# A step of two elements in the stationary operand of an up projection's matmuls

## The chip, the cores and the metric

The kernel runs on one core of a Trainium2 chip. The metric is the device time of one execution in microseconds (us). TensorE (PE) does the matmuls and, as instructions of their own, the loads of the stationary operand (PEld in the profile); VectorE is DVE, ScalarE is ACT, GpSimd is POOL, SyncE is SP.

## The reference

The program is two layers of an encoder on 256 tokens of width 2048. Each layer is an input projection, two kinds of attention, an output projection, and then the part that this case is about, a gated feed-forward block of width 5632:

```python
D_MODEL = 2048; SEQ = 256; DEPTH = 2; D_FF = 5632
def depthwise_conv(u, w, bias):
    up = jnp.pad(u, ((0, 0), (1, 1), (0, 0)))
    return up[:, :-2] * w[0] + up[:, 1:-1] * w[1] + up[:, 2:] * w[2] + bias
...
for l in range(DEPTH):
    h = rms_norm(x, ln1_g[l])
    proj = h @ w_in[l]
    ...                                  # two groups of attention heads
    x = x + o @ w_out[l]
    h2 = rms_norm(x, ln2_g[l])
    u = depthwise_conv(h2 @ w_up[l], conv_w[l], conv_b[l])
    gate, up = u[..., :D_FF], u[..., D_FF:]
    x = x + (jax.nn.silu(gate) * up) @ w_down[l]
```

All arrays are float32. `w_up` is 2048 x 11264: its first 5632 columns give the gate, the others the value that is gated.

## The kernel before, in words

**Numbers in two parts.** TensorE reads float32 operands in a type called float32r here. To keep the precision, every operand is split into a high part (the value written as float32r, by ACT) and a low part (the rest, by DVE). A product is then taken as high x high + low x high + high x low.

**Quanta and steps.** The weights come from DRAM in quanta of 128 partitions x 2048 float32. A quantum is worked on in steps, of which each takes a half of 1024 elements a partition: SP issues a DMA into a tile `raw`, ACT writes the high part `whi` from it (line 1002), DVE the low part `wlo` (line 1011); for some halves a DMA that adds, issued by POOL, makes the low part in the tiles `v_a` and `v_b` instead (line 988). Some high parts lie in a tile named `kT`. All of these copies go over the 1024 elements in a row, whatever they mean. Splits run four steps ahead of the matmuls.

**The up projection.** For each of 44 blocks f of 128 columns (of the gate and of the value) there are two quanta u, so four steps; in two layers 2 x 44 x 4 = 352 steps. One step holds, for four blocks kk of 128 input rows, the 128 columns of the gate (j = 0) and the 128 columns of the value (j = 1). `q_up` gives TensorE 8 pairs of matmuls in a step, one pair for each j and kk. In a pair the weights are the stationary operand and the tile `xs` is the moving one; `xs` holds the high part of 128 input rows x 256 tokens and behind it the low part. The function `two` makes the pair: high weights with all 512 columns of `xs` (128 x 512), then low weights with the 256 columns of its high part (128 x 256). So a step is 16 matmuls, each with a load of its own, and the widths 512 and 256 alternate. The stationary operand is 128 partitions x 128 float32, before the change in a row (512 bytes of a partition).

**Other matmuls.** The input, output and down projections have activations as stationary and weights as moving operand, 512 columns wide throughout (`three`, `q_seven`, `q_plain`, `q_down`).

**What sets the order.** In the feed-forward part the class `Plan` puts the operations of ACT, DVE, POOL and PE in order from costs and due times that stand in the code; outside it a scheduler does. Both go by sizes and not by where a matmul reads its operands. After the up matmuls of a block, `glu` on ACT and DVE reads the sums from PSUM and does the convolution, the gate and the splits.

**Where the weights lie.** `place` puts the split weights of an up step 56 elements into their tile (`UP_AT`). `_layout` arranges the weights on the host, ahead of the run.

Of the kernel before, what the change touches and what calls it, by code (L numbers as in the profile page):

```python
# [18 lines left out]
P = 128  # L19
L = 2  # L20
# [11 lines left out]
NF = FF // P  # L32
# [94 lines left out]
def encoder_kernel(  # L127
# [370 lines left out]
    def two(ps, w_h, w_l, mv, first, last):  # L498

        mm(ps, w_h, mv, first, False)  # L500
        mm(ps[:, 1], w_l, mv[:, 0], False, last)
# [121 lines left out]
    def q_up(l, f, u):  # L623
        def body(q, half, hi, lo):
            if u == 0 and half == 0:
                cur["up"] = psum.tile([P, 2, 2, T], F32, name="mm", bufs=2)
            ps = cur["up"]
            hv, lv = (w.rearrange("p (k j n) -> p k j n", k=4, j=2) for w in (hi, lo))
            for j in range(2):
                for kk in range(4):  # L630
                    k = 8 * u + 4 * half + kk
                    two(ps[:, j], hv[:, kk, j], lv[:, kk, j], xs[k], k == 0, k == KD - 1)
            if u == 1 and half == 1:
                glu(l, f, q, ps)
        return body
# [247 lines left out]
    for l in range(L):  # L883
# [7 lines left out]
        f = 0  # L891
# [363 lines left out]
def _layout(inputs):  # L1255
    f = {k: np.asarray(v) for k, v in inputs.items()}
    c = np.ascontiguousarray
    o = {}
    rows = T // GRID_W

    down = np.arange(T).reshape(rows, GRID_W).T.reshape(-1)
    o["x"] = c(f["x"][0][down].reshape(TT, P, D).transpose(1, 0, 2))
    o["xT"] = c(f["x"][0][down].T.reshape(KD, P, T).transpose(1, 0, 2))
    o["pos"] = c(f["positions"][down].reshape(TT, P).T)
    d = HD
    inv = np.float32(10000.0) ** (-np.arange(0, d, 2, dtype=np.float32) / np.float32(d))
    o["inv"] = inv.astype(np.float32)
    ln_g = np.stack([f["ln1_g"], f["ln2_g"]]).reshape(2, L, KD, P).transpose(3, 0, 1, 2)
    o["head"] = c(np.concatenate([ln_g.reshape(P, -1), o["xT"][:, :2].reshape(P, -1)], 1))
    o["qk_g"] = c(np.stack([f["qn_a"], f["kn_a"], f["qn_b"], f["kn_b"]], 1))  # L1270
    o["sink"] = c(f["sink"].reshape(-1))
    o["on_g"] = c(np.stack([f["on_a"], f["on_b"]], 1).reshape(L, 2, NH, P).transpose(3, 0, 1, 2))
    conv = np.concatenate([f["conv_w"], f["conv_b"][:, None]], 1)
    o["conv"] = c(conv.reshape(L, 4, 2 * NF, P).transpose(3, 0, 1, 2))
    w = f["w_in"]
    qa, ka, va, qb = (w[:, :, i * 1024:(i + 1) * 1024] for i in range(4))
    kvb = w[:, :, 4096:]
    h = slice(0, 512), slice(512, 1024)
    js = {"kvb": kvb, "qb0": qb[..., h[0]], "qb1": qb[..., h[1]], "va0": va[..., h[0]], "va1": va[..., h[1]],
          "ka0": ka[..., h[0]], "ka1": ka[..., h[1]], "qa0": qa[..., h[0]], "qa1": qa[..., h[1]]}  # L1280
    wi = np.stack([js[j] for j in JOBS], 1)
    o["w_in"] = c(wi.reshape(L, NJ, 4, 4, P, 512).transpose(0, 1, 2, 4, 3, 5)).reshape(L, NJ, 4, P, 2048)
    o["w_out"] = c(f["w_out"].reshape(L, 2, 2, 4, P, NB, 512).transpose(0, 1, 5, 2, 4, 3, 6)).reshape(
        L, 2, NB, 2, P, 2048)
    o["w_up"] = c(f["w_up"].reshape(L, 2, 8, P, 2, NF, P).transpose(0, 5, 1, 3, 2, 4, 6)).reshape(
        L, NF, 2, P, 2048)
    wd = f["w_down"]
    n = NF // PART

    four = wd[:, :n * PART * P].reshape(L, n, PART // 2, 2, P, 2, 2, 512).transpose(0, 1, 5, 2, 3, 4, 6, 7)  # L1290
    o["w_seven"] = c(np.stack([four[:, :, :, :, k, :, m] for k, m in ((1, 1), (0, 0), (0, 1), (1, 0))], 5)).reshape(
        L, n, 2, PART // 2, P, 2048)
    o["w_plain"] = c(four[:, :, :, :, 1, :, 0].transpose(0, 1, 2, 4, 3, 5)).reshape(L, n, 2, P, 2048)
    o["w_down"] = c(f["w_down"].reshape(L, NF // FG, FG, P, NB, 512).transpose(0, 1, 4, 3, 2, 5)).reshape(
        L, NF // FG, NB, P, 2048)

    r, cc = np.arange(T) // GRID_W, np.arange(T) % GRID_W
    wr = min(WIN_R, rows)
    r0 = np.clip(r - wr // 2, 0, rows - wr)
    c0 = np.clip(cc - WIN_C // 2, 0, GRID_W - WIN_C)  # L1300
    inside = ((cc[None] >= c0[:, None]) & (cc[None] < c0[:, None] + WIN_C)
              & (r[None] >= r0[:, None]) & (r[None] < r0[:, None] + wr))
    dr = np.clip(r[None] - r[:, None], -(WIN_R - 1), WIN_R - 1) + WIN_R - 1
    dc = np.clip(cc[None] - cc[:, None], -(WIN_C - 1), WIN_C - 1) + WIN_C - 1
    bias = np.full((L, NH, T, T), NEG, np.float32)
    bias[:, :, inside] = f["rpb"][:, :, dr[inside], dc[inside]]

    bias = bias[:, :, down][:, :, :, down]
    bias = np.stack([bias[:, :, tt * P:(tt + 1) * P, tt * (T - KW):tt * (T - KW) + KW] for tt in range(TT)], 2)
    o["bias"] = c(bias.transpose(0, 1, 3, 2, 4))  # L1310
    i = np.arange(T)
    mb = np.where(np.abs(i[:, None] - i[None]) <= WINDOW, np.float32(0), np.float32(NEG))
    mb = mb[down][:, down]
    o["mask_b"] = c(mb.reshape(TT, P, T).transpose(1, 0, 2).astype(np.float32))
    return o
# [19 lines left out]
```

## Time and profile before

| | |
|---|---|
| median of 3 runs (lowest to highest) | 2070.07 us (2069.88 to 2070.23) |
| the profiled execution | 2070.64 us, its span 2068.9 us |
| PE, busy share of the span | 100% |
| PEld, DVE, ACT, POOL | 86%, 82%, 75%, 8% |
| granted TensorE clock | 1.000 |

Matmuls are pipelined, and the profile models their ends, so that PE's share says only that it never stands long without work. The distance from one matmul's start to the next one's tells what one costs. Loads (PEld) overlap the matmuls; a load's recorded duration holds its latency too, so that two loads can overlap each other in the record.

### The profile page before, as it was taken

What the parts mean: (1) busy time and instruction counts of PE and PEld (TensorE: products, weight loads), DVE (VectorE), ACT (ScalarE), POOL (GpSimd) and SP (SyncE); (2) the same over time, 40 slices, a digit from 0 to 9 for tenths busy, and PEclk for the clock granted to TensorE, in tenths of its full rate; (3) what the DMA queues carried; (4) which work ended last, traced back from release to release, by engine and by line L of the source; (5) the groups of instructions that cost most, each with busy time, mean ns of one, the idle gap of its engine ahead of it and who ended that gap; (6) DMA issues with size and microseconds to landing.
All of it is one profiled execution on the core that took longest, in us unless ns stands there. A gap on an engine that the chain in (4) does not pass through costs nothing.

```text
span 2068.9 us, 30510 instructions
## 1 busy us (share of the span) xinstructions
PE 2062.4 (100%) x10720; PEld 1769.9 (86%) x10720; DVE 1706.1 (82%) x2576; ACT 1549.3 (75%) x2595; POOL 157.6 (8%) x170
## 2 busy tenths in 40 slices
PE   9999999999999999999999999999999999999999
PEld 8888888888888888888888888888888888888887
DVE  7786655889999999999757866558899999999995
ACT  7566646988888888888555665479888888888883
POOL 0011000000000000000000111000000000000000
PEclk9999999999999999999999999999999999999999
DMA  9655557888888888898655555678788888888883
GB/s 350 204 163 163 171 180 200 256 233 249 256 265 251 257 251 259 250 263 255 219 181 177 173 166 164 191 211 242 239 251 258 254 256 264 256 252 259 253 261 131
DMA packets 134009, 472.48 MB, mean 228 GB/s; under 512 B 15328, under 2 KB 17888, under 8 KB 133856
## 3 DMA queue, kind: packets, MB, share of 16 engines
q1 hardware_dynamic: 117872, 413.87, 61.2%
q0 software_dynamic: 15264, 55.58, 15.0%
q8 instruction: 84, 1.38, 0.3%
q10 hardware_dynamic: 720, 1.08, 0.2%
q14 instruction: 69, 0.57, 0.1%
HBM read 412.80 MB, written 2.10 MB: 201 GB/s over the span
## 4 chain that ended last, share of the span: by engine, by line
PE 99%; DMA 0%; ACT 0%; ACTq 0%; DVE 0%; issue 0%
PE mm L165 85%; PE S L165 6%; PE pv L165 4%; PE tr L165 3%; PE tr L460 1%; PE tr L381 1%; PE S L220 1%; DMA mid<-in_xT 0%; ACT v_a L335 0%; ACT whi L1002 0%; ACT mid L182 0%; ACT xs L182 0%; DVE x L872 0%; ACTq L1105 0%; ACTq L1098 0%
## 5 line engine op out<-in xcount | busy, mean ns | idle before, releaser
L165 PE MATMUL mm<-xs,whi 128*128 128x512 f32 x2320 | 810.0, 390 | 0.0
L1011 DVE TENSOR_TENSOR wlo<-raw,whi 128x1024 fp32r<-128x1024 f32 x503 | 613.0, 1220 | 185.0 <-ACT whi L1002 162.4
L1002 ACT ACTIVATE whi<-raw 128x1024 fp32r<-128x1024 f32 x569 | 596.2, 1055 | 222.2 <-PE mm L165 182.8
L165 PE MATMUL mm<-xs,wlo 128*128 128x256 f32 x2112 | 596.2, 282 | 0.0
L165 PEld LDWEIGHTS mm<-xs,whi 128*128 128x128 f32 x2320 | 435.3, 188 | 92.1 <-ACT prob L651 0.6
L165 PEld LDWEIGHTS mm<-xs,wlo 128*128 128x128 f32 x2112 | 399.0, 189 | 3.7
L165 PE MATMUL mm<-whi,xs 128*128 128x512 f32 x1152 | 294.8, 393 | 0.8 <-ACT whi L179 0.7
L165 PE MATMUL mm<-whi,mid 128*128 128x512 f32 x928 | 255.2, 393 | 0.4 <-ACT v_a L335 0.4
L165 PEld LDWEIGHTS mm<-whi,xs 128*128 128x128 f32 x1152 | 212.7, 188 | 43.5 <-ACT whi L179 1.3
L165 PEld LDWEIGHTS mm<-whi,mid 128*128 128x128 f32 x928 | 169.9, 188 | 34.3 <-ACT v_a L335 0.9
L165 PE MATMUL mm<-xs,kT 128*128 128x512 f32 x496 | 174.6, 390 | 0.0
L165 PE MATMUL mm<-wlo,xs 128*128 128x512 f32 x576 | 158.7, 392 | 0.0
L667 ACT ACTIVATE pT<-halo,conv 128x256 f32<-128x256 f32 x352 | 157.8, 498 | 0.0
L165 PE MATMUL mm<-wlo,mid 128*128 128x512 f32 x486 | 152.7, 393 | 0.0
L651 ACT ACTIVATE prob<-mm 128x512 f32<-128x512 f32 x176 | 103.6, 591 | 50.2 <-PE mm L165 49.8
L692 DVE TENSOR_TENSOR pT<-pT 128x512 f32<-128x512 f32 x176 | 120.8, 686 | 10.7 <-ACT pT L665 4.3
L165 PEld LDWEIGHTS mm<-wlo,xs 128*128 128x128 f32 x576 | 107.1, 188 | 21.5
L165 PEld LDWEIGHTS mm<-xs,kT 128*128 128x128 f32 x496 | 93.1, 188 | 19.5
L165 PEld LDWEIGHTS mm<-wlo,mid 128*128 128x128 f32 x486 | 90.9, 188 | 19.1
L665 ACT ACTIVATE pT<-halo,conv 128x256 f32<-128x256 f32 x176 | 103.7, 590 | 0.0
L165 PE MATMUL mm<-xs,v_a 128*128 128x256 f32 x352 | 99.3, 282 | 0.0
L165 PE MATMUL mm<-xs,v_b 128*128 128x256 f32 x352 | 99.3, 282 | 0.0
(251 smaller groups left out, 3043.1 us busy)
## 6 DMA issues: line engine op xcount, KB each, us to landing
raw<-in_w_up SPq DMA_DIRECT2D x262, 512.0 KB, 5.6
raw<-in_w_in SPq DMA_DIRECT2D x142, 512.0 KB, 4.4
raw<-in_w_seven SPq DMA_DIRECT2D x110, 512.0 KB, 5.9
raw<-in_w_out SPq DMA_DIRECT2D x64, 512.0 KB, 3.8
tabs<-in_w_up SPq DMA_DIRECT2D x48, 512.0 KB, 5.7
aux<-in_w_up SPq DMA_DIRECT2D x42, 512.0 KB, 5.5
v_a<-raw POOLq DMA_DIRECT2D x39, 512.0 KB, 6.5
v_b<-raw POOLq DMA_DIRECT2D x39, 512.0 KB, 6.5
```

Of the source, the lines that this page charges most:

```text
L165: nc.tensor.matmul(ps, lhsT, rhs, start=start, stop=stop, skip_group_check=True)
L220: nc.tensor.transpose(ps[:, j, tt * P:(tt + 1) * P], x[:, tt, (k + j) * P:(k + j + 1) * P], ident)
L381: nc.tensor.transpose(ps[:, j, tt * P:(tt + 1) * P], qn[tt][:, p + j, :], ident)
L460: nc.tensor.transpose(ps[:, kt, tt * P:(tt + 1) * P], p[:, tt, kt * P:(kt + 1) * P], ident)
L651: nc.scalar.activation(own[part], ps[:, :, part], AF.Copy)
L665: nc.scalar.activation(own["y"][:, j], src, AF.Identity, scale=taps[j][i], bias=taps[j][3])
L667: nc.scalar.activation(own[name][:, j], src, AF.Copy, scale=taps[j][i])
L692: lambda n=n: nc.vector.tensor_add(own["y"], own["y"], own[n]),
L1002: highs[s] = nc.scalar.activation(his[s], source(s), AF.Copy)
L1011: nc.vector.tensor_sub(los[s], source(s), his[s].bitcast(F32))
```

## The change

In the host's layout, the 256 elements that hold one block kk in a half were 128 columns of the gate and behind them 128 of the value. Now they are gate, value, gate, value, in turns. `q_up` reads its operands accordingly: the stationary operand of j starts at element j of the 256 and goes on in steps of two elements (8 bytes), over 1024 bytes of a partition in place of 512.

```diff
@@ q_up
             ps = cur["up"]
-            hv, lv = (w.rearrange("p (k j n) -> p k j n", k=4, j=2) for w in (hi, lo))
+            hv, lv = (w.rearrange("p (k n j) -> p k j n", k=4, j=2) for w in (hi, lo))
             for j in range(2):
                 for kk in range(4):
                     k = 8 * u + 4 * half + kk
                     two(ps[:, j], hv[:, kk, j], lv[:, kk, j], xs[k], k == 0, k == KD - 1)
@@ _layout
-    o["w_up"] = c(f["w_up"].reshape(L, 2, 8, P, 2, NF, P).transpose(0, 5, 1, 3, 2, 4, 6)).reshape(
+    o["w_up"] = c(f["w_up"].reshape(L, 2, 8, P, 2, NF, P).transpose(0, 5, 1, 3, 2, 6, 4)).reshape(
         L, NF, 2, P, 2048)
```

The built program has the same instructions in the same order on every engine, PE, DVE, ACT, POOL and SP. The products, and the order in which they are added up, are the same. What differs is the step of the stationary operand in the up projection's matmuls and the order of the numbers in `in_w_up`.

## The prediction

> **What bounds the kernel.** I read the page first: the shares of the engines, the granted clock by slices, and the shares of the chain that ended last.
>
> ```profile
> span 2068.9 us, 30510 instructions
> ...
> PE 2062.4 (100%) x10720; PEld 1769.9 (86%) x10720; DVE 1706.1 (82%) x2576; ACT 1549.3 (75%) x2595; POOL 157.6 (8%) x170
> ...
> PEclk9999999999999999999999999999999999999999
> ...
> PE 99%; DMA 0%; ACT 0%; ACTq 0%; DVE 0%; issue 0%
> ```
>
> PE carries 99% of the chain, at the full clock in every slice: what a matmul costs decides, and nothing else does while DVE (82%) and ACT (75%) keep up. Loads are as many as matmuls, 10720.
>
> Next, how many of them the change touches. The groups by line and shape of PEld show the up projection's loads as those with `xs` beside a tile that holds weights; `kT`, `v_a` and `v_b` hold such weights too in these stages.
>
> ```profile
> L165 PEld LDWEIGHTS mm<-xs,whi 128*128 128x128 f32 x2320 | 435.3, 188 | 92.1 <-ACT prob L651 0.6
> L165 PEld LDWEIGHTS mm<-xs,wlo 128*128 128x128 f32 x2112 | 399.0, 189 | 3.7
> ...
> L165 PEld LDWEIGHTS mm<-xs,kT 128*128 128x128 f32 x496 | 93.1, 188 | 19.5
> ...
> L165 PEld LDWEIGHTS mm<-xs,v_a 128*128 128x128 f32 x352 | 66.5, 189 | 0.0
> L165 PEld LDWEIGHTS mm<-xs,v_b 128*128 128x128 f32 x352 | 66.5, 189 | 0.0
> ```
>
> High weights: 2320 + 496 = 2816. Low weights: 2112 + 352 + 352 = 2816. That is 352 steps x 8 pairs, by the code too; 5632 loads in all. A recorded 188 ns with its latency doesn't say what a load holds up, so I looked at starts in the timeline, here one pair of an up step:
>
> ```profile
> 340.06 0.39 PE L165 MATMUL mm<-xs,whi 128*128 128x512 f32 x1
> 340.06 0.19 PEld L165 LDWEIGHTS mm<-xs,wlo 128*128 128x128 f32 x1
> 340.29 0.28 PE L165 MATMUL mm<-xs,wlo 128*128 128x256 f32 x1
> 340.29 0.19 PEld L165 LDWEIGHTS mm<-xs,whi 128*128 128x128 f32 x1
> 340.41 0.39 PE L165 MATMUL mm<-xs,whi 128*128 128x512 f32 x1
> ```
>
> The load of the low weights starts together with the 512-wide matmul and has 0.23 us until its own matmul starts; the load of the high weights starts with the 256-wide matmul and has only 0.12 us. So a high load has the thin cover.
>
> Exact distances come from long pieces of the chain, in which PE went from matmul to matmul without a wait (start, length, what):
>
> ```profile
> 10.30 65.60 PE mm L165 x288
> ...
> 75.90 0.44 PE tr L381 x4
> ...
> 338.70 81.25 PE mm L165 x468
> ```
>
> The first is the input projection, 512 columns wide throughout: 65.60 / 288 = 227.8 ns a matmul. The last is the up projection: 468 matmuls are 234 pairs, 81.25 / 234 = 347.2 ns a pair. So a 256-wide matmul takes 347.2 - 227.8 = 119.4 ns.
>
> **The change part by part.** It removes and adds no instruction and moves none: the order on all five engines is the same. DMAs bring the same bytes in the same pieces. The two copies that split the weights go over 1024 elements in a row, as before:
>
> ```profile
> L1011 DVE TENSOR_TENSOR wlo<-raw,whi 128x1024 fp32r<-128x1024 f32 x503 | 613.0, 1220 | 185.0 <-ACT whi L1002 162.4
> L1002 ACT ACTIVATE whi<-raw 128x1024 fp32r<-128x1024 f32 x569 | 596.2, 1055 | 222.2 <-PE mm L165 182.8
> ```
>
> Their 1220 and 1055 ns stay, so those terms are zero. If PE gets slower they only wait longer for free tiles (182.8 us of ACT's idle time there is already a wait for PE); if it gets faster, ACT's 75% and DVE's 82% leave room for some per cent. The whole question is what the 5632 loads cost when they go over 1024 bytes of a partition in steps of 8.
>
> *Term 1, the load beside its cover.* How long does a load occupy its path? The nearest row is where matmuls one column wide follow each other, so that only the loads are left:
>
> ```profile
> 248.45 0.55 PEld L165 LDWEIGHTS pv<-ones,acc_b 128*128 128x128 f32 x4
> ...
> 248.91 0.30 PEld L165 LDWEIGHTS S<-kT,qT 128*128 128x128 f32 x2
> ```
>
> Four loads in 248.91 - 248.45 = 0.46 us, 115 ns each. (These are plain f32 loads; the float32r ones have the same 188 ns in the record, and I take 115 for them too.) Beside 119.4 ns that leaves 4 ns. Lower end: the load takes one element in each of its cycles whether they touch or not, and nothing changes, 0. Upper end: it takes twice as long, 230 ns, and sticks out by 230 - 119.4 = 111 ns under each of 2816 256-wide matmuls, 311 us, and by 2 ns under the 512-wide ones, 6 us: +317 us. Between them I go by pace: the moving operand of a 512-wide matmul is 2048 bytes of a partition in 227.8 ns, 9.0 bytes a ns, so that TensorE does read at this pace; 1024 bytes in 115 ns are 8.9. The strided load asks for no more than the moving operand gets. I take 0 for this term.
>
> *Term 2, what a load takes from the matmul it lies under.* Is the matmul beside a load slower? From 512 to 256 columns the distance falls by 227.8 - 119.4 = 108.4 ns, 0.423 ns a column; 512 columns are then 216.8 ns, and 11.0 ns of each matmul do not depend on its width. A second stretch, of neighbouring down and up matmuls, gives the same by other rows:
>
> ```profile
> 412.86 0.39 PE L165 MATMUL mm<-xs,whi 128*128 128x512 f32 x1
> ...
> 418.41 0.39 PE L165 MATMUL mm<-xs,whi 128*128 128x512 f32 x1
> ...
> 419.79 0.62 PE L165 MATMUL tr<-kT,mid 128*128 128x512 f32 x2
> ...
> 422.96 0.40 PE L165 MATMUL mm<-wlo,mid 128*128 128x512 f32 x1
> ```
>
> Sixteen pairs in 5.55 us are 346.9 ns each; 14 matmuls of 512 columns in 3.17 us are 226.4; so 120.5 for 256 columns, 0.414 a column and 14.6 left over. I take 13 ns, between the two. What is it? In the four transposes of the chain above, 128 columns in plain f32, a matmul with its load takes 0.44 / 4 = 110 ns, hardly more than a one-column matmul with its load (115): there the columns run at half the pace and no remainder shows. So a load is not dear in itself; the remainder stands where the moving operand streams at its full 9 bytes a ns. I read it as what the load's reads of memory take from that stream. If so, it goes with the stretch of memory that a load touches, and 1024 bytes in place of 512 take another 13 ns. Lower end: the remainder has another cause, or goes by the count of elements, 0; below nothing, it could shrink to none, -13 ns (third rival). [...] I take the doubling, nearest to the row: it only follows the bytes.
>
> *The sum.* 5632 x 13 ns = +73 us, on the profiled execution 2070.64 (its span 2068.9 and 1.7 around it) 2143.9; that execution is 0.6 above the median of 2070.07, so against the median 2143. The path takes all of it, for PE is on the chain throughout. What is late next is nothing: ACT, DVE and the DMAs get 13 x 16 = 208 ns more for each up step.
>
> [...]
>
> **Rivals.**
>
> *No change, 2070.* The 13 ns are a fixed price of changing the weights, or go by elements, and the load stays under its 119.4 ns. For it: a load is 128 elements before and after, and the plain f32 rows show that loads can lie fully beside matmuls. Against it: the remainder is only there beside the fast stream, and 4 ns of slack is little.
>
> *The load outgrows its cover, 2190 to 2390.* It decides from 119.4 ns on; each further 10 ns under the 2816 narrow matmuls costs 28 us, up to 2070 + 317 = 2387 when the load takes double. For it: 115 beside 119.4. Against it: the pace of 8.9 bytes a ns that the moving operand reaches.
>
> *Faster, down to 2008.* Two reads that collide by their places in memory may collide less. Now the load goes through memory at half the pace of the moving operand (512 bytes in 115 ns, 4.5 a ns against 9.0) and they cross again and again; with the step both go at 9 and could keep apart. In the transposes both streams are equally fast (512 bytes in 110 ns each), and the remainder is missing. If it fell from 13 to 2 ns: -11 x 5632 = -62 us, 2008. It takes a remainder under 13 to decide, at any size. Against it: equal pace can also mean colliding all the time.
>
> That the change doesn't do what it says is excluded: every one of the up projection's matmuls has the step in the built program.
>
> **How the numbers follow.** The remainder grows by about its own size (2100 to 2190): 0.39. It grows a little (2074 to 2100): 0.06. No change: 0.30. The load outgrows its cover: 0.16, half of it under 2260. Faster: 0.09. The likeliest is 2143. The range runs from 2066 (no change, and a little below) to 2260: it leaves out the faster case and half of the long load, 0.17. A measurement of this kernel tells about 0.2% (4 us) from no change. Slower 0.39 + 0.06 + 0.16 = 0.61, the same 0.30, faster 0.09.
>
> **What would show it.** In the timeline of after, a pair of the up projection at 0.373 us in place of 0.347, with both distances longer by 13 ns; input projection pieces still at 227.8 ns; ACT's wait for PE ahead of `whi` longer, its 1055 ns and DVE's 1220 unchanged. No change would show as 0.347 again. A long load would show in the distance from the 256-wide matmul to the next alone: 0.12 would become 0.19 or more, and the other would stay at 0.23. I am wrong in the mechanism if one distance alone moves, and in the sign if pairs get shorter.

## The result, and the profile after

The changed kernel takes 2092.49 us, the kernel before 2070.15 beside it: the ratio is 1.0107, with an interval from 1.0089 to 1.0124. That is 22.3 us more, slower as forecast, but less than a third of the 73 us that I expected.

The page of the changed kernel, the lines that answer to those of before:

```profile
span 2090.8 us, 30510 instructions
...
PE 2084.8 (100%) x10720; PEld 1794.1 (86%) x10720; DVE 1706.6 (82%) x2576; ACT 1551.8 (74%) x2595; POOL 157.6 (8%) x170
...
PEclk9999999999999999999999999999999999999999
...
PE 99%; DMA 0%; ACT 0%; ACTq 0%; DVE 0%; issue 0%
...
L1011 DVE TENSOR_TENSOR wlo<-raw,whi 128x1024 fp32r<-128x1024 f32 x503 | 612.9, 1220 | 188.2 <-ACT whi L1002 164.7
L1002 ACT ACTIVATE whi<-raw 128x1024 fp32r<-128x1024 f32 x569 | 596.3, 1056 | 228.7 <-PE mm L165 172.4
```

DVE and ACT have the same busy time and the same 1220 and 1056 ns an instruction; PE is still the whole chain (99%) at the full clock (granted 1.000). The loads of the up projection have a longer record, 197 ns in place of 188:

```profile
L165 PEld LDWEIGHTS mm<-xs,whi 128*128 128x128 f32 x2320 | 456.8, 197 | 88.1
L165 PEld LDWEIGHTS mm<-xs,wlo 128*128 128x128 f32 x2112 | 415.6, 197 | 2.6
...
L165 PEld LDWEIGHTS mm<-xs,kT 128*128 128x128 f32 x496 | 97.7, 197 | 18.8
```

The same two pieces of the chain (start, length, what):

```profile
10.34 65.60 PE mm L165 x288
...
338.90 82.80 PE mm L165 x468
```

The input projection is as it was, 227.8 ns a matmul. In the up projection 234 pairs take 82.80 us, 353.8 ns a pair in place of 347.2: 6.6 ns more, times 2816 pairs 18.6 us of the 22.3. One pair in the timeline:

```profile
346.27 0.40 PE L165 MATMUL mm<-xs,whi 128*128 128x512 f32 x1
346.28 0.20 PEld L165 LDWEIGHTS mm<-xs,wlo 128*128 128x128 f32 x1
346.51 0.28 PE L165 MATMUL mm<-xs,wlo 128*128 128x256 f32 x1
346.51 0.20 PEld L165 LDWEIGHTS mm<-xs,whi 128*128 128x128 f32 x1
346.63 0.40 PE L165 MATMUL mm<-xs,whi 128*128 128x512 f32 x1
```

From the wide matmul to the narrow one it is now 0.24 us (0.23 before), from the narrow to the wide one 0.12 as before. (The means over the trace's 2810 and 2742 distances of the two kinds within the up projection are 228.6 ns before and 235.7 after, and 118.6 and 117.9.)

### The profile page after: what moved, and what is told of

It reads as the page before. It is cut to its first block, busy times and chain, and to the rows that moved or that the text cites. A ratio compares the mean times of both kernels' runs of the same rounds, so it can differ in the third digit from the quotient of the medians.

```text
span 2090.8 us, 30510 instructions
## 1 busy us (share of the span) xinstructions
PE 2084.8 (100%) x10720; PEld 1794.1 (86%) x10720; DVE 1706.6 (82%) x2576; ACT 1551.8 (74%) x2595; POOL 157.6 (8%) x170
## 4 chain that ended last, share of the span: by engine, by line
PE 99%; DMA 0%; ACT 0%; ACTq 0%; DVE 0%; issue 0%
PE mm L165 85%; PE S L165 6%; PE pv L165 4%; PE tr L165 3%; PE tr L460 1%; PE tr L381 1%; PE S L220 1%; DMA mid<-in_xT 0%; ACT v_a L335 0%; ACT whi L1002 0%; ACT mid L182 0%; ACT xs L182 0%; DVE x L872 0%; ACTq L1105 0%; ACTq L1098 0%
## 5 line engine op out<-in xcount | busy, mean ns | idle before, releaser
L165 PE MATMUL mm<-xs,whi 128*128 128x512 f32 x2320 | 825.1, 398 | 0.0
L1011 DVE TENSOR_TENSOR wlo<-raw,whi 128x1024 fp32r<-128x1024 f32 x503 | 612.9, 1220 | 188.2 <-ACT whi L1002 164.7
L1002 ACT ACTIVATE whi<-raw 128x1024 fp32r<-128x1024 f32 x569 | 596.3, 1056 | 228.7 <-PE mm L165 172.4
L165 PEld LDWEIGHTS mm<-xs,whi 128*128 128x128 f32 x2320 | 456.8, 197 | 88.1
L165 PEld LDWEIGHTS mm<-xs,wlo 128*128 128x128 f32 x2112 | 415.6, 197 | 2.6
L165 PEld LDWEIGHTS mm<-xs,kT 128*128 128x128 f32 x496 | 97.7, 197 | 18.8
```

Source lines behind the costliest of these rows:

```text
L165: nc.tensor.matmul(ps, lhsT, rhs, start=start, stop=stop, skip_group_check=True)
L1002: highs[s] = nc.scalar.activation(his[s], source(s), AF.Copy)
L1011: nc.vector.tensor_sub(los[s], source(s), his[s].bitcast(F32))
```

## The experiments

Two theories stood against each other. **Clash**, as the forecast had it: the strided load takes reads from the moving stream of the matmul that it lies under, above all the load of the low weights under the wide matmul, whose distance grew. **Late load**, my second rival at a small size: the strided load of the high weights outlasts its thin cover under the narrow matmul; if a matmul's recorded start comes before its wait for its weights, as `e13_narrow_192_row` below has it (0.09 us up to the wide one's start, 0.25 from it to the next), the delay shows in the next distance, the one that grew. In what follows a pair's time is always the up projection's long piece of the chain over its 234 pairs (235 or 241.5 where the piece is longer); in every run at full clock the second layer has the same piece with the same length.

**One load at a time (`e1_hi_strided`, `e2_lo_strided`).** On the changed kernel:

```diff
-            hv, lv = (w.rearrange("p (k n j) -> p k j n", k=4, j=2) for w in (hi, lo))
+            hv, lv = (w.rearrange("p (%s) -> p k j n" % o, k=4, j=2) for w, o in ((hi, "k n j"), (lo, "k j n")))
```

and with the two orders exchanged.

> The high weights are read with a step of two, the low weights in a row (so the low weights go to the wrong columns; the time is what is looked at). After the change the 512-wide distance went from 228.6 to 235.7 ns and the 256-wide one from 118.6 to 117.9. Theory 'clash': the strided load of the low weights, which lies under the 512-wide matmul, takes more from its moving stream; then this kernel is as before, 2070 us (2068 to 2073), 512-wide at 0.228 us. Rival 'late load': the strided load of the high weights, under the 256-wide matmul, outlasts its cover of 118 ns by some 7 ns, and since a matmul's start is recorded when it begins to read, the delay shows in the next distance; then this kernel has nearly all of the loss, 2088 to 2093 us.

> The other half: the low weights are read with a step of two, the high weights in a row (so the high weights go to the wrong columns). 'Clash' expects the whole loss here, 2088 to 2093 us, with 0.236 us for the 512-wide matmul. 'Late load' expects 2070 us (2068 to 2073).

2081.65 us (ratio 1.0054, interval 1.0039 to 1.0069) and 2073.05 (1.0014, 1.0005 to 1.0024); pairs of 351.6 and 347.3 ns. The piece of the chain with the high weights strided:

```profile
338.60 82.27 PE mm L165 x468
```

and with the low weights:

```profile
338.86 81.26 PE mm L165 x468
```

The high weights alone have 11 us, the low weights alone under 3, so the load under the narrow matmul is the dear one. But neither expectation holds: the two add up to 14, and both together cost 22. Both kernels have the new order of the numbers in `in_w_up`, so that order by itself, without the step in the high weights, costs under 3 us.

**A step of four (`e3_step_four`).** Four operands in turns:

```diff
-            hv, lv = (w.rearrange("p (k n j) -> p k j n", k=4, j=2) for w in (hi, lo))
+            hv, lv = (w.rearrange("p (k n i j) -> p k i j n", k=2, i=2, j=2) for w in (hi, lo))
...
-                    two(ps[:, j], hv[:, kk, j], lv[:, kk, j], xs[k], k == 0, k == KD - 1)
+                    two(ps[:, j], hv[:, kk // 2, kk % 2, j], lv[:, kk // 2, kk % 2, j], xs[k], k == 0, k == KD - 1)
...
-    o["w_up"] = c(f["w_up"].reshape(L, 2, 8, P, 2, NF, P).transpose(0, 5, 1, 3, 2, 6, 4)).reshape(
+    o["w_up"] = c(f["w_up"].reshape(L, 2, 4, 2, P, 2, NF, P).transpose(0, 6, 1, 4, 2, 7, 3, 5)).reshape(
```

> All loads of the up projection with a step of four elements (16 bytes, 2048 bytes of a partition a load), four operands in turns. 'Clash' by pieces of memory: twice as many 16-byte pieces once more, 512-wide matmuls 7 to 15 ns longer again, 2110 to 2140 us. 'Late load' at a fixed pace of 9 bytes a ns: 2048 bytes take 227 ns, 109 over the cover of 118, times 2816, +307 us, 2377 us (2300 to 2400). If a load's time goes by elements alone: no more than after, 2092 us.

2402.58 us (1.1604, 1.1585 to 1.1623).

```profile
341.69 109.11 PE mm L165 x468
```

109.11 / 234 = 466.3 ns a pair: just above late load's range and far from the other two. A load's time does go by what it touches (by itself, as measured below, 111.6 ns in a row, 117.8 with a step of two and 233 with one of four), and a step of four makes it the limit.

**Loads by themselves (`e7_short_row`, `e8_short_step`, `e12_short_four`).** Both matmuls of a pair 64 columns wide, on the kernels with steps of one, two and four:

```diff
-        mm(ps, w_h, mv, first, False)
-        mm(ps[:, 1], w_l, mv[:, 0], False, last)
+        mm(ps if first else ps[:, 0, 0:64], w_h, mv if first else mv[:, 0, 0:64], first, False)
+        mm(ps[:, 1, 0:64], w_l, mv[:, 0, 0:64], False, last)
```

> Control for the next run: the kernel before with both matmuls of a pair 64 columns wide, but for the first one of each sum (so most of the up projection's products are left out). 64 columns take 27 ns, so loads are all that is left: 112 to 116 ns from matmul to matmul within a step. The time is bounded by ACT and DVE then and isn't looked at.

> The same with the step of two. If a load in steps is longer by itself (part of 'late load'): 120 to 125 ns from matmul to matmul. If it is longer only because the moving stream is read beside it: 112 to 116 ns as in the control.

> Loads alone (both matmuls of a pair 64 columns wide, but for the first one of each sum, so most products are left out), with the step of four. Where the clock is full, 112 ns were measured in a row and 118 to 120 with the step of two. The run with a step of four at full width had pairs of 465 ns; by 'late load' a pair is the 228 of the wide matmul and a whole load, so a load is 237 ns here (225 to 245). If its length came from the moving stream beside it: 112 to 130 ns.

In these runs the granted clock fell to a half in stretches (its mean was 0.81, 0.80 and 0.76); I read loads in a row and in steps of two from stretches of full clock. In a row, the first and the last matmul of such a stretch, 38 distances:

```profile
462.06 0.27 PE L165 MATMUL mm<-xs,whi 128*128 128x64 f32 x1
...
466.30 0.31 PE L165 MATMUL mm<-xs,whi 128*128 128x64 f32 x1
```

and with a step of two, 36 distances:

```profile
515.85 0.28 PE L165 MATMUL mm<-xs,whi 128*128 128x64 f32 x1
...
520.09 0.28 PE L165 MATMUL mm<-xs,whi 128*128 128x64 f32 x1
```

4.24 / 38 = 111.6 ns and 4.24 / 36 = 117.8 ns: the strided load is 6.2 ns longer with next to nothing beside it, a little less than the 120 to 125 ns that I expected. The stretches' clock stands third from the end in the views by window, 1.00 in both (the columns ahead are the busy times and counts of the engines):

```profile
462.00:466.30 4.30, 4.30 (x41) 4.27 (x39) 4.16 (x8) 3.88 (x8) 0.00 (x0) 1.00 0.50 162
```

```profile
515.80:520.00 4.20, 4.20 (x38) 4.18 (x36) 4.06 (x7) 3.30 (x6) 0.86 (x1) 1.00 0.53 199
```

With a step of four, 14 distances take 3.26 us, 233 ns each, here at half clock (0.50):

```profile
346.10 0.42 PE L165 MATMUL mm<-xs,wlo 128*128 128x64 f32 x1
...
349.36 0.42 PE L165 MATMUL mm<-xs,whi 128*128 128x64 f32 x1
```

```profile
346.00:350.00 4.00, 4.00 (x19) 4.00 (x18) 0.00 (x0) 0.00 (x0) 0.00 (x0) 0.50 0.22 86
```

The same trace has stretches of full clock, and there 14 distances take 3.26 us too:

```profile
461.98 0.40 PE L165 MATMUL mm<-xs,whi 128*128 128x64 f32 x1
...
465.24 0.40 PE L165 MATMUL mm<-xs,whi 128*128 128x64 f32 x1
```

```profile
461.98:465.24 3.26, 3.26 (x16) 3.26 (x16) 3.15 (x5) 2.84 (x4) 0.00 (x0) 1.00 0.47 161
```

So the step of four doesn't go by TensorE's clock, and twice 233 is its pair at full width (466.3): there both loads are the limit. The other two do go by the clock. At half clock the up projection's first long piece has the same 458 matmuls in the same 101.12 us with loads in a row and with a step of two:

```profile
338.75:439.87 101.12, 101.12 (x459) 99.57 (x459) 61.24 (x92) 71.36 (x131) 6.12 (x7) 0.50 0.69 197
```

```profile
341.26:442.38 101.12, 101.12 (x459) 99.58 (x459) 58.67 (x88) 70.50 (x129) 6.12 (x7) 0.50 0.66 191
```

Between two matmuls of 64 columns the distance is 213 ns there in both, 1.9 times the 111.6 of full clock. So a load seems to have two limits, one that goes with the clock (111.6 ns at full clock, 213 at half) and one that goes with what it touches and not with the clock (233 ns with a step of four at both); the step of two brings the second just over the first (117.8 beside 111.6), at full clock only (213 in both at half).

**A load as the limit (`e13_narrow_192_row`, `e14_narrow_192_step`, `e17_narrow_192_hi`, `e18_narrow_192_lo`).** The narrow matmul 192 columns wide, with loads in a row, both strided, and the high or the low ones alone strided (by the edits of `e1_hi_strided` and `e2_lo_strided`); one execution each:

```diff
-        mm(ps[:, 1], w_l, mv[:, 0], False, last)
+        mm(ps[:, 1, 0:192], w_l, mv[:, 0, 0:192], False, last)
```

> The kernel before with the narrow matmul of a pair only 192 columns wide (a quarter of the low x high product is left out). Without a limit by the load a pair would fall by 64 x 0.417 = 26.7 ns to 320. 'Late load': a load in a row lasts 112 ns and the narrow matmul gives a cover of only some 92, so the pair stops at wide matmul plus load, 228 + 112 = 340 ns (336 to 345). If loads under the narrow matmul set nothing: 320.

> The same with the step of two. 'Late load': wide matmul plus a load of 118 to 120 ns, 228 + 119 = 347 ns a pair, 6 to 8 over the control. If the strided load costs by taking reads from the moving stream and not by its length: the control's pair plus some 3 (the narrow stream is shorter), or 327 where nothing waits for loads.

> Narrow matmul 192 columns wide, only the high weights read with the step of two, the low weights in a row (wrong columns for them). A pair's floor was 340.1 ns with both in a row and 352.8 with both strided. If the floor is the wide matmul plus the load of the high weights, and the strided load is 6 to 8 ns longer by itself while the rest is what the strided load of the low weights takes from the wide matmul: 346 to 349 ns here. If the load of the high weights makes up all of the 12.7 ns: 352 to 353.

> The other half: only the low weights with the step of two. If what the strided load of the low weights takes from the wide matmul above it is a part of its own (5 ns, as between the two kernels with all matmuls 512 wide and the weights at 64): 344 to 346 ns a pair. If the load of the high weights makes up everything: 340.

(The 340.1 and 352.8 in the third are means over the whole trace; the table goes by the long piece.) The long piece of the chain, in a row:

```profile
338.47 79.72 PE mm L165 x468
```

both strided:

```profile
338.71 82.75 PE mm L165 x468
```

high weights strided:

```profile
338.64 82.01 PE mm L165 x468
```

low weights strided:

```profile
338.54 80.72 PE mm L165 x468
```

| step of two in | 192 columns, ns a pair | 256 columns, ns a pair | 256 columns, us |
|---|---|---|---|
| none | 340.7 | 347.2 | 2070.15 |
| low weights | 345.0 | 347.3 | 2073.05 |
| high weights | 350.5 | 351.6 | 2081.65 |
| both | 353.6 | 353.8 | 2092.49 |

The control stops at 340.7 where its columns alone would let it go to 320: 227.8 of the wide matmul and 112 of a load, as late load said. This is a floor under the pair, and the step raises it by 4.3 ns through the low weights' load, 9.8 through the high weights' and 12.9 through both. Only the first and the last expectation hold: I had given both strided 6 to 8 ns over the control, and the high ones 346 to 349 or 352 to 353. Of the 9.8 ns, 6.2 are the length of the load by itself; where the other 3.6 come from isn't shown. And now the right column follows from the left one: a pair takes the larger of its floor and the 347.2 ns of its columns. Larger of 345.0 and 347.2: 347.2 (347.3 measured). 350.5: 350.5 (351.6). 353.6: 353.6 (353.8). That is why the two halves did not add up: 6.5 ns of slack are used up once, whichever comes first.

In the timeline of `e13_narrow_192_row` one sees where a late load is recorded:

```profile
346.25 0.41 PE L165 MATMUL mm<-xs,whi 128*128 128x512 f32 x1
346.50 0.25 PE L165 MATMUL mm<-xs,wlo 128*128 128x192 f32 x1
346.59 0.41 PE L165 MATMUL mm<-xs,whi 128*128 128x512 f32 x1
```

The narrow matmul's own distance is 0.09 us, its columns alone; the wait for the load stands in the wide one's, 0.25 where 0.23 is usual. So here the late load lengthened the distance behind the matmul that waited for it, not the one of the matmul that covered it.

**Every load under a wide matmul (`e9_full_row`, `e10_full_step`, and with the weights 64 elements into their tile `e15_full_row_start_64`, `e16_full_step_start_64`).**

```diff
-        mm(ps[:, 1], w_l, mv[:, 0], False, last)
+        mm(ps, w_l, mv, False, last)
...
-UP_AT = 56
+UP_AT = 64
```

(the second part in the latter two).

> Control for the next run. The kernel before, with the low weights' matmul over all 512 columns of xs too (one small product more, the sums stay right): every load of the up projection now lies under a 512-wide matmul. A pair is twice 227 to 228 ns, 2816 pairs 301 to 310 us more: 2371 to 2381 us.

> The changed kernel (step of two) with the low weights' matmul over all 512 columns. 'Late load': a strided load is 118 to 120 ns long and now always has 227 ns of cover, so it costs nothing: within 4 us of the control. 'Clash' with the moving stream of 512-wide matmuls, 7.1 ns for each: 20 to 40 us over the control.

> The control with both matmuls of a pair 512 wide and loads in a row, with the up weights 64 elements into their tile in place of 56 (32 bytes further, as the operands of the other projections lie). If the extra of 12.7 ns a pair in the control (466.7 against 454) comes from where the two reads lie in memory: 454 ns, some 2372 us. If not: 466.7 again, 2406 us.

> The same with the step of two. 'Late load': a strided load of 118 to 120 ns has 227 ns of cover, so within 4 us of its control. 'Clash': 20 to 40 us over it.

At 56 the two are 2406.33 and 2408.54 us, 2.2 apart, and I first took that for late load alone. But the control is 25 us and more over what I expected of it; its piece of the chain:

```profile
338.14 112.66 PE mm L165 x483
```

112.66 / 241.5 = 466.5 ns a pair. At 64 it is nearly there, 2378.73, and the strided kernel stays at 2407.61 (one execution each). The long piece at 64, in a row:

```profile
337.58 110.38 PE mm L165 x483
```

and strided:

```profile
337.72 112.59 PE mm L165 x483
```

110.38 / 241.5 = 457.1 and 466.2 ns a pair, 29 us in all. The 457.1 is a mixture. `UP_AT` moves `whi`, `kT` and `wlo`, but not the low weights in `v_a` and `v_b`, a quarter of them, which a transfer makes at the start of their tiles and `place` doesn't touch. In a row, 24 pairs with `wlo` and then 8 with `v_b`:

```profile
344.82 0.39 PE L165 MATMUL mm<-xs,whi 128*128 128x512 f32 x1
...
355.70 0.40 PE L165 MATMUL mm<-xs,whi 128*128 128x512 f32 x1
...
359.43 0.39 PE L165 MATMUL mm<-xs,kT 128*128 128x512 f32 x1
```

and the same pairs strided:

```profile
345.01 0.39 PE L165 MATMUL mm<-xs,whi 128*128 128x512 f32 x1
...
356.20 0.40 PE L165 MATMUL mm<-xs,whi 128*128 128x512 f32 x1
...
359.93 0.39 PE L165 MATMUL mm<-xs,kT 128*128 128x512 f32 x1
```

In a row that is 10.88 / 24 = 453.3 ns, the 454 that I expected, and 3.73 / 8 = 466; strided it is 466 in both. So where both weights start at 64, a strided load costs the wide matmuls 6.5 ns each, with cover to spare (117.8 ns by itself under 227). A late load can't do that. So a loss as clash had it does exist; that it is reads taken from the moving stream isn't shown. Where the low weights stayed in their place, and everywhere at 56, the all-wide pairs have the loss with loads in a row too, and the step adds nothing. What about the place makes it, and whether the 4.3 ns of the low weights above are the same loss, isn't shown: the kernel before has its weights at 56 as well, and its wide matmuls take 228.6 ns and not 233.

**Places (`e4_start_48`, `e11_row_start_48`).** `UP_AT = 48` in the changed kernel and in the kernel before:

> The changed kernel with the up weights 48 elements into their tile in place of 56, so 32 bytes earlier, all else as after. 'Clash' by where the two reads are in memory: the 512-wide distance moves by several ns in one direction or the other, 2080 to 2105 us and not 2092. 'Late load' goes by the number of bytes and pieces, which a shift of 32 bytes hardly changes: 2090 to 2095 us.

> The kernel before (loads in a row) with the up weights 48 elements into their tile in place of 56, the control for the shifted start in steps of two, which cost 33 us. If the shift is dear for itself, whatever the step: 2080 to 2090 us. If a load in a row of 112 ns has room for it under 118: 2068 to 2074 us.

2103.78 us (1.0161, 1.0146 to 1.0176) and 2079.50 (1.0042, 1.0027 to 1.0057). 32 bytes cost 9 us with loads in a row and 11 with the step. The first lies in clash's 2080 to 2105 and not in late load's 2090 to 2095; the second lies between its two ranges, just under the 2080 of "dear for itself". The place matters beside the step, about half as much (9 to 11 us beside 22), and I didn't find by what rule.

**A wider narrow matmul (`e5_wide_row`, `e6_wide_step`).** 288 columns:

```diff
-        mm(ps[:, 1], w_l, mv[:, 0], False, last)
+        mm(ps.rearrange("p j t -> p (j t)")[:, 224:512], w_l, mv.rearrange("p j t -> p (j t)")[:, 0:288], False, last)
```

> Control for the next run. The kernel before, with the narrow matmul of each pair 288 columns wide in place of 256 (32 columns of the low part more, so the sums are others). 32 columns at 0.417 ns are 13.3 ns, 2816 times +37.6 us: 2107 to 2109 us by every theory, if the load is covered before already. If the load under the narrow matmul was what set the 118.6 ns before, less: 2085 to 2100.

> The changed kernel (step of two) with the narrow matmul 288 columns wide. 'Late load': the cover is now 131 ns, more than a load some 7 ns longer than 118 needs, so the loss is gone: within 4 us of the control with loads in a row. 'Clash': the load goes on taking reads from the moving stream, so the loss stays, 18 to 24 us over the control.

2128.09 (1.0276, 1.0259 to 1.0293) and 2129.55 us (1.0283, 1.0267 to 1.0298), 1.5 apart. It looks like late load, but the control has 7 ns a pair more than its columns explain, in which a loss can hide, so I don't count it. Where these 7 ns come from stays open. It also shows a border of the rule above: here, and with all matmuls wide at 56, a pair with loads in a row takes more than the larger of its floor and its columns.

## Why the prediction was right or wrong

- **No instruction moved, ACT, DVE and DMAs as before, PE takes all of it:** right.
- **Term 1, the load beside its cover, taken as 0:** this step failed first. I argued that a strided load asks for no more bytes a ns than the moving operand gets; by itself it is 6.2 ns longer all the same, and under the narrow matmul 9.8. The rival that a load outgrows its cover is what happened, but, with what the low weights' loads add, at 18.6 us: far below its 2190 to 2390, of which the upper end had 317. My slack of 4 ns was a little small: a pair had 347.2 - 340.7 = 6.5.
- **Term 2, what a load takes from the matmul, +13 ns for each of 5632 loads:** this step made the sum too large. A loss of this kind exists, but for a strided load under a wide matmul it is 4.3 ns (192 columns), 6.5 ns (all wide, at 64) or nothing (all wide, at 56). Doubling the remainder because the bytes double was wrong; a third to a half of it came on top. And I charged it in full, where the slack of a pair swallows it first: with the low weights alone strided a pair took 347.3 ns beside 347.2. That the remainder belongs to the fast stream is borne out by a stretch of `e7_short_row` at half clock (0.50), where 9 distances of 512 columns in the down projection take 3.84 us, 426.7 ns: twice 213.3, so that the 227 of full clock have 13 to 14 ns that go with the fast stream alone. That it is the load's reads that take them isn't shown.

```profile
454.95 0.63 PE L165 MATMUL mm<-wlo,mid 128*128 128x512 f32 x1
...
458.79 0.63 PE L165 MATMUL S<-wlo,mid 128*128 128x512 f32 x1
```

```profile
454.95:458.79 3.84, 3.84 (x11) 2.97 (x9) 2.47 (x5) 2.62 (x4) 0.00 (x0) 0.50 1.01 290
```

- **The sum:** 26 ns a pair forecast; 12.9 raised the floor, 6.5 were slack, 6.6 came out (with the 0.2 between floor and measurement). 2816 x 6.6 = 18.6 us.
- **The rest, 3.7 us, isn't settled.** It lies among matmuls that the change didn't touch, at the same places in memory. The step in the high weights doesn't make it: by the same reckoning the run with the high weights strided has -1 us of it (11.2 less 2816 x 4.4 ns). The 14 down matmuls that took 3.17 us before (419.79 to 422.96) take 3.21 after:

```profile
421.54 0.62 PE L165 MATMUL tr<-kT,mid 128*128 128x512 f32 x2
...
424.75 0.39 PE L165 MATMUL mm<-wlo,mid 128*128 128x512 f32 x1
```

- **What would show it:** I wrote that one distance alone moving would mean a wrong mechanism, and one alone did move; but I had placed a long load in the distance behind the narrow matmul, and it is recorded in the next (0.24 us in place of 0.23, with 0.12 behind the narrow one as before).
- **The range** (2066 to 2260) holds 2092; the likeliest value was off by 51 us. "It grows a little", 2074 to 2100, had 0.06 from me.

## What to carry to other kernels

In these runs a load and the matmul above it ran side by side, and a pair with 256 columns took about the larger of its columns (347.2 ns) and of the floor that its loads set (345.0, 350.5 and 353.6 with steps of two): measure the slack (make the narrow matmul narrower until the time stops falling; here one width, 192, was run) before charging a slower load, and charge only what exceeds it. With loads at 112 ns beside 118, a step of two cost 1% and a step of four 16%. When the distance from one matmul to the next grows, ask whether the first of the two waited for its weights: in `e13_narrow_192_row` the wait stands in the 0.25 us behind the wide matmul, which waited, and the narrow one that covered the load shows 0.09.

## What the runs showed of the hardware

- A load of 128 float32 columns took 111.6 ns in a row, 117.8 with a step of 8 bytes and 233 with one of 16 (`e7_short_row`, `e8_short_step`, `e12_short_four`): 1.06 and 2.1 times the load in a row. 233 / 128 = 1.82 ns an element. By the bytes that a load goes over this is 1024 / 117.8 = 8.7 bytes a ns with the step of 8 and 2048 / 233 = 8.8 with the step of 16, beside 512 / 111.6 = 4.6 in a row: the two strided loads went at one pace. In what pieces they read isn't shown. At half clock a load takes 213 ns in a row and with a step of 8 bytes, and still 233 with one of 16.
- 32 bytes in the place of the stationary operand moved this kernel by 9 us (0.4%) with loads in a row, and the all-wide pair, where both its weights moved, from 466.5 to 453.3 ns.
